# First expert of a mixture of experts: row numbers ahead of the gates, one-hots between the weights' second parts

## The chip, the cores and the metric

The kernel runs on one core of a Trainium2 chip. A core has TensorE (PE), VectorE (DVE), ScalarE (ACT), GpSimd (POOL) and SyncE (SP), each with its own line of instructions that it works off in order, and 16 DMA engines that move data between HBM and the core's own memory (SBUF). Matrix products go to PSUM. The metric is the device time of the whole program in microseconds (us).

## What is computed

A diffusion backbone of two layers over 1024 tokens of width 1024. Layer 0 mixes tokens by attention, layer 1 by a Fourier transform; behind each stands a mixture of experts: each token picks one of four groups, and in it two of eight experts, so there are 32 experts and 2048 pairs of a token and an expert. Cut to that part:

```python
lg = xt @ w_rg + b_rg                       # 4 groups
g_sel = argmax(lg); p_grp = max(softmax(lg))
le_sel = (xt @ w_re + b_re) of group g_sel  # 8 experts
top_l, top_i = top_k(le_sel, 2)
gate = p_grp * softmax(top_l)
y[t] = sum over both e of gate * ((silu(x @ w1[e]) * (x @ w3[e])) @ w2[e])
x = x + g2 * y
```

All inputs are float32.

## The kernel before, in words

**Gathering an expert's rows.** The routing (`route_part`, L1078) leaves for every token and expert a place among that expert's tokens (`posb`), and a table `val` of five small numbers: two make up the token's row number (written early by GpSimd), three are the gate weight in three bfloat16 parts (VectorE, L1168 to L1171). `slot_index` (L1206) makes for one expert a one-hot matrix `oneh` of 1024 tokens by 104 slots (VectorE, L1216), multiplies it with `val` on TensorE (`pi`, L1219), and reads from the product the row numbers (`row`, `idx`) and the gates (`gate`). With `idx` GpSimd gathers 104 rows of the normed input H from HBM (`xg`, L1333). H is stored row tile by row tile on SyncE's queue, the last tile on ScalarE's (L1024). `xin` (L1337) transposes the rows (`pt`) and splits them into a first part `xh` (ScalarE) and a second part `xl` = `pt` - `xh` (VectorE, L1346).

**Weights.** Each expert has twelve weight quarters of 128 x 1024 numbers: four of w1, four of w3, four of w2. A quarter comes by SyncE's queue, is split by ScalarE into `wh` (L1264) and by VectorE into `wl` = weight - `wh` (L1269); there are five buffers for split quarters, and quarters are split three ahead of their use. Every product is then three matmuls (`mm3`): first parts (L211), `wl` with `xh` (L212), `wh` with `xl` (L213). Before the experts start, eleven halves of weight matrices are loaded and the first five quarters' `wh` are cast; their five `wl` are left for later ("late", L1279) and done by `finish_late`.

**The start of the experts** (`phase_moe`). `prep(0, 1)` makes the one-hot, row numbers and gate of expert 0 and its gather is issued. TensorE does 14 products of no use on the one-hot meanwhile (`keep_warm`, L218). A `behind` marker on GpSimd behind the gather holds VectorE back from the next: `finish_late` does the five late `wl`, `prep(1, 3)` the one-hots and row numbers of experts 1 to 3, then `xin` of expert 0. Expert 0's products for w1 (`h1`) and w3 (`h3`) follow; between them `xin` of expert 1 and `prep(4, 4)`. VectorE multiplies both (`gg`, L1367). Expert 1 then runs like every later one: h1, `gg` of expert 0 transposed and split (`gh`, `gl`), w2's product of expert 0 (`py`), h3.

The order within an engine's line comes from the order in which the program issues, which a scheduler changes by its own estimate; `issue_after` and `behind` tie an instruction behind another one. The gain V of layer 1's first norm (`next_norm`, L1411, V = (V + 1) * norm gain) is computed ahead of layer 0's experts. `route_extra` (around 924 us) looks for experts with more than 104 rows.

Of the kernel before, what the change touches and what calls it, by code (L numbers as in the profile page):

```python
# [209 lines left out]
def mm3(nc, out, lh, ll, wh, wl, start, stop):  # L210
    nc.tensor.matmul(out, lh, wh, start=start, stop=False)  # L211
    nc.tensor.matmul(out, lh, wl, start=False, stop=False)  # L212
    nc.tensor.matmul(out, ll, wh, start=False, stop=stop)  # L213

# [861 lines left out]
def route_part(g, m, n0, n1, buf=None, pt_=None):  # L1076
# [6 lines left out]
    with ExitStack() as st:  # L1083
        if buf is None:
            wk = g.pool(st, "ra", 1)
            pp = g.pool(st, "rap", 1, psum=True)
# [53 lines left out]
        V.tensor_copy(m.posb[:, ns], m.posm[:, ns])  # L1140
        ex = T("ex", N, NG)
        V.tensor_tensor(ex, lg[:, :, 0], gm.to_broadcast([P, N, NG]), OP.subtract)
        nc.scalar.activation(ex, ex, AF.Exp)
        V.tensor_sub(m2, m2, m1)
        V.tensor_mul(m2, m2, ohg)
        e2 = T("e2", N)
        V.reduce_sum(e2, m2, axis=AX.X)
        nc.scalar.activation(e2, e2, AF.Exp)
        for oh in (oh1, oh2):
            V.tensor_mul(oh, oh, ohg[:, :, :, None].to_broadcast(sh))  # L1150
        o1, o2 = (oh.rearrange("p t g e -> p t (g e)") for oh in (oh1, oh2))
        pg = T("pg", N)
        V.reduce_sum(pg, ex, axis=AX.X)
        V.reciprocal(pg, pg)
        w1 = T("w1", N)
        V.tensor_scalar(w1, e2, 1.0, None, OP.add)
        V.reciprocal(w1, w1)
        V.tensor_mul(w1, w1, pg)
        w2 = T("w2", N)
        V.tensor_mul(w2, w1, e2)  # L1160

        val = m.val[:, ns]
        sh = [P, N, NE]
        V.tensor_mul(o1, o1, w1[:, :, None].to_broadcast(sh))
        V.tensor_mul(o2, o2, w2[:, :, None].to_broadcast(sh))
        G = o1
        V.tensor_add(G, o1, o2)
        V.tensor_copy(val[:, :, :, 2], G)  # L1168
        V.tensor_sub(G, G, val[:, :, :, 2])
        V.tensor_copy(val[:, :, :, 3], G)  # L1170
        V.tensor_sub(val[:, :, :, 4], G, val[:, :, :, 3])  # L1171
        if n1 == NT:
            m.cnt = m.one.tile([P, NE], F32, name="cnt")
            V.tensor_copy(m.cnt, cnt)

# [29 lines left out]

def slot_index(g, m, wk, pp, n, posm, val, tag):  # L1206

    nc = g.nc
    b = NE // 4 - 1 if n > 3 else 1
    pi = pp.tile([CAP, n, 5], F32, name="pi")  # L1210
    for e in range(n):
        oh = wk.tile([P, NT, CAP], BF, name="oneh", bufs=3)
        pe = posm(e)
        for t0, t1 in ((0, NT),) if n > 1 else ((0, NT - 2), (NT - 2, NT)):
            sh = [P, t1 - t0, CAP]
            nc.vector.tensor_tensor(oh[:, t0:t1], g.jrow[:, None, :].to_broadcast(sh),  # L1216
                                    pe[:, t0:t1, None].to_broadcast(sh), OP.is_equal)
        for t in range(NT):
            i = nc.tensor.matmul(pi[:, e], oh[:, t], val(e, t), start=(t == 0), stop=(t == NT - 1)).ins  # L1219
    g.slots = i, oh.rearrange("p t c -> p (t c)")[:, :512]  # L1220
    row = wk.tile([CAP, n], F32, name="row" + tag, bufs=1)
    nc.vector.tensor_scalar(row, pi[:, :, 1], float(SEQ), None, OP.add)
    idx = wk.tile([CAP, n], I32, name="idx" + tag, bufs=b)
    g.idx = nc.vector.tensor_add(idx, row, pi[:, :, 0]).ins
    gate = wk.tile([CAP, n], F32, name="gate" + tag, bufs=b)
    nc.vector.reduce_sum(gate, pi[:, :, 2:5], axis=AX.X)
    return idx, gate


class Moe:  # L1230
# [44 lines left out]

    def finish_late(self):

        for l, t, h in self.late:
            self.vsub = self.g.nc.vector.tensor_sub(l, t, h).ins  # L1279
        self.late = []  # L1280
        self.feed()
# [55 lines left out]
    def xin(self, xg):  # L1337
        g, nc = self.g, self.g.nc
        xh = self.wk.tile([P, KD, CAP], F32R, name="xh")
        xl = self.wk.tile([P, KD, CAP], F32R, name="xl")  # L1340
        for q in range(2):
            pt = self.ps.tile([P, 4, CAP], F32, name="pt", bufs=2)
            for j in range(4):
                nc.tensor.transpose(pt[:, j], xg[:, (4 * q + j) * P:(4 * q + j + 1) * P], g.ident[:CAP, :CAP])  # L1344
            nc.scalar.copy(xh[:, 4 * q:4 * q + 4], pt)  # L1345
            nc.vector.tensor_sub(xl[:, 4 * q:4 * q + 4], pt, xh[:, 4 * q:4 * q + 4])  # L1346
        return xh, xl
# [4 lines left out]
    def mm(self, out, x, piece, i, n=0, kpp=2):  # L1352

        hv, lv = (t.rearrange("p (k n) -> p k n", k=kpp)[:, :, n * 512:(n + 1) * 512] for t in piece)
        for j in range(kpp):
            k = i * kpp + j
            mm3(self.g.nc, out, x[0][:, k], x[1][:, k], hv[:, j], lv[:, j], k == 0, k == 4 * kpp - 1)

# [43 lines left out]
    def next_norm(self):  # L1402

        g, nc = self.g, self.g.nc
        if self.l:
            with g.tc.issue_after(self.piece):
                bcast_row(g, self.V, g.a["final_norm"].rearrange("(o d) -> o d", o=1), nc.sync)
            return
        bcast_row(g, self.G2, g.a["norm_mix"][1:2], nc.sync)
        bcast_row(g, self.V, g.mod[1][0:1, D:2 * D], nc.sync)  # L1410
        nc.vector.scalar_tensor_tensor(self.V, self.V, 1.0, self.G2, OP.add, OP.mult)  # L1411
        self.tab = {}

    def table(self, n):
# [25 lines left out]
def phase_moe(g, mo, after=None, fin=None):  # L1440
# [4 lines left out]
    with mo.st as st:  # L1445
# [12 lines left out]

        prep(0, 1)
        gather(0)  # L1460
        first = mo.last.ins
        with tc.issue_after(g.slots[0]):
            keep_warm(g, mo.psum("py", 2), g.slots[1], NWARM[0])
# [687 lines left out]
```

## Time and profile before

| | us |
|---|---|
| median of 3 runs | 2293.72 |
| lowest and highest | 2289.53, 2297.05 |
| the profiled execution, by the device's own time | 2295.38 |
| its span, first to last instruction | 2293.6 |
| TensorE busy in it | 2115.9 (92%) |
| VectorE busy in it | 1905.6 (83%) |
| ScalarE, GpSimd busy in it | 1341.7 (58%), 1014.5 (44%) |

The mean granted clock of TensorE is 0.964 of full. Layer 0's experts begin near 856 us of the span, layer 1's near 1643. A row of a timeline begins with the start and the busy time in us, then engine, line, operation, result <- inputs, shape, and the count where like instructions in a row are printed as one; in brackets stands the idle time ahead of it and what ended that. Engines overlap the end of one operation with the start of the next, so the busy time of one is some tenths longer than its share in a row.

### The profile page before, as it was taken

The numbers are of one execution on the slowest core, as the hardware profiler recorded it, in microseconds if no ns is written. First come the engines' busy times: TensorE is split into PE (matmuls) and PEld (weight loads), VectorE is DVE, ScalarE is ACT, GpSimd is POOL, SyncE is SP. The second block draws the span as 40 slices with busy tenths as digits, with TensorE's granted clock in tenths as the row PEclk, the third lists the DMA queues.
The fourth block names the chain that finished last, engine by engine and source line by source line (L and its number), as shares of the span: only waits on it lengthen the run. The fifth ranks groups of instructions, "written<-read, shape, count | busy, mean of one in ns | idle before, by whom it ended". The sixth has DMA issues, their size and how long they took to land. (4 is left out here: it accounts for less than half of the span.)

```text
span 2293.6 us, 29597 instructions
## 1 busy us (share of the span) xinstructions
PE 2115.9 (92%) x10301; PEld 1435.9 (63%) x10301; DVE 1905.6 (83%) x2782; ACT 1341.7 (58%) x1745; POOL 1014.5 (44%) x546
## 2 busy tenths in 40 slices
PE   6899899999999869999999999799699999999993
PEld 3677454444545656677777776457476777777662
DVE  4878566666677889999999999656899999999995
ACT  4743444444444236777777777543487777776774
POOL 3322577777778532334433443313223334434433
PEclk9999899999999989999999999899899999999997
DMA  8545533534335778999999999654699999999995
GB/s 304 190 156 157 174 119 126 177 118 138 120 107 177 269 270 284 364 368 335 364 361 337 370 378 327 218 228 167 243 329 351 377 311 370 366 354 361 355 354 198
DMA packets 152070, 612.13 MB, mean 267 GB/s; under 512 B 26928, under 2 KB 43960, under 8 KB 105916
## 3 DMA queue, kind: packets, MB, share of 16 engines
q1 hardware_dynamic: 109628, 544.77, 64.3%
q0 software_dynamic: 24672, 54.40, 9.3%
q10 hardware_dynamic: 17616, 11.01, 1.5%
q8 instruction: 83, 1.36, 0.2%
q14 instruction: 71, 0.58, 0.1%
HBM read 557.47 MB, written 77.39 MB: 277 GB/s over the span
## 5 line engine op out<-in xcount | busy, mean ns | idle before, releaser
L212 PE MATMUL h<-wl,xh 128*104 128x512 f32 x1024 | 409.3, 400 | 16.5 <-DVE wl L1269 15.4
L211 PE MATMUL h<-wh,xh 128*104 128x512 f32 x1024 | 408.8, 400 | 0.5 <-ACT xh L1345 0.5
L213 PE MATMUL h<-wh,xl 128*104 128x512 f32 x1024 | 406.6, 397 | 0.0
L572 DVE TENSOR_REDUCE m<-sm 128x1 f32<-128x512 f32 x360 | 201.8, 593 | 107.6 <-PE sm L571 107.1
L1333 POOL DMA_INDIRECT xg<-H,idx x64 | 106.0, 1656 | 287.7 <-PE pt L1344 170.2
L212 PEld LDWEIGHTS h<-wl,xh 128*104 128x104 f32 x1024 | 173.4, 169 | 85.8 <-DVE wl L1269 24.3
L1264 ACT CAST wh<-raw 128x1024 fp32r<-128x1024 f32 x196 | 200.2, 1056 | 32.7 <-PE h L213 20.8
L1269 DVE TENSOR_TENSOR wl<-raw,wh 128x1024 fp32r<-128x1024 f32 x175 | 212.7, 1255 | 6.9 <-ACT wh L1264 6.8
L1269 DVE TENSOR_TENSOR wl<-wl,wh 128x1024 fp32r<-128x1024 f32 x163 | 211.0, 1323 | 2.5 <-ACT wh L1264 1.9
L211 PEld LDWEIGHTS h<-wh,xh 128*104 128x104 f32 x1024 | 173.3, 169 | 61.5 <-ACT xh L1345 0.9
L213 PEld LDWEIGHTS h<-wh,xl 128*104 128x104 f32 x1024 | 173.5, 169 | 60.7
L1388 POOL DMA_INDIRECT Xs<-y,idx x64 | 177.1, 2768 | 71.9 <-DVE y L1387 42.9
L1269 DVE TENSOR_TENSOR wl<-wh 128x1024 fp32r<-128x1024 f32 x157 | 206.4, 1337 | 3.0 <-ACT wh L1264 2.4
L1264 ACT CAST wh<-wh 128x1024 fp32r<-128x1024 f32 x180 | 186.3, 1054 | 38.2 <-PE h L213 26.7
L212 PE MATMUL py<-wl,gh 128*104 128x512 f32 x512 | 203.9, 399 | 0.1
L213 PE MATMUL py<-wh,gl 128*104 128x512 f32 x512 | 201.6, 396 | 0.5 <-DVE gl L1378 0.4
L1264 ACT CAST wh<-wl 128x1024 fp32r<-128x1024 f32 x172 | 178.4, 1055 | 34.7 <-PE h L213 24.8
L211 PE MATMUL py<-wh,gh 128*104 128x512 f32 x512 | 196.5, 402 | 2.0 <-ACT gh L1377 1.8
L1264 ACT CAST wh<-X 128x1024 fp32r<-128x1024 f32 x124 | 129.5, 1054 | 52.7 <-PE h L213 41.3
L1269 DVE TENSOR_TENSOR wl<-X,wh 128x1024 fp32r<-128x1024 f32 x113 | 141.4, 1283 | 4.2 <-ACT wh L1264 4.1
L1269 POOL TENSOR_TENSOR wl<-wh 128x1024 fp32r<-128x1024 f32 x23 | 67.3, 2926 | 166.3 <-issue 95.0
L571 PE MATMUL sm<-KS,qs 128*128 128x512 f32 x360 | 135.4, 383 | 0.0
(576 smaller groups left out, 4710.0 us busy)
## 6 DMA issues: line engine op xcount, KB each, us to landing
raw<-in_moe_w_dram SPq DMA_DIRECT2D x98, 1024.0 KB
wh<-in_moe_w_dram SPq DMA_DIRECT2D x90, 1024.0 KB
wl<-in_moe_w_dram SPq DMA_DIRECT2D x86, 1024.0 KB
qs<-in_moe_w_dram SPq DMA_DIRECT2D x96, 512.0 KB
raw<-in_w_mod_dram SPq DMA_DIRECT2D x43, 1024.0 KB
X<-in_moe_w_dram SPq DMA_DIRECT2D x37, 1024.0 KB
X<-in_moe_w_dram SPq DMA_DIRECT2D x50, 512.0 KB
QS<-qst ACTq DMA_DIRECT2D x32, 256.0 KB
```

The costliest lines, as they stand in the source:

```text
L211: nc.tensor.matmul(out, lh, wh, start=start, stop=False)
L212: nc.tensor.matmul(out, lh, wl, start=False, stop=False)
L213: nc.tensor.matmul(out, ll, wh, start=False, stop=stop)
L571: nc.tensor.matmul(ps[:, :kn], qs[:, h, qt * P:(qt + 1) * P], g.KS[:, g4, k0:k0 + kn], start=True, stop=True)
L572: nc.vector.reduce_max(m3[:, h, qt, b:b + 1], ps[:, :kn], axis=AX.X)
L1264: nc.scalar.copy(h, t)
L1269: i = (nc.gpsimd if pool else nc.vector).tensor_sub(l, t, h)
L1333: self.last = self.g.nc.gpsimd.indirect_dma_start(out=xg, out_offset=None, in_=self.H if src is None else src, in_offset=bass.IndirectOffs ...
L1388: return y, lambda: nc.gpsimd.indirect_dma_start(out=self.X, out_offset=bass.IndirectOffsetOnAxis(ap=idx, axis=0), in_=y, in_offset=None, ...
```

## The change

Six edits, all around the start of the experts.

1. In `route_part` the gate weights become a function of their own, called for the last stretch of tokens after the first gather is issued; the `cnt` copy goes to ScalarE. The routing's buffers stay open through the experts.
2. `slot_index` can make row numbers only (`rows_only`): a product with two columns of `val`, then `idx`; the gate comes from a second product with the other three columns, on the same one-hot.
3. `finish_late(2)` does two late `wl`, then come expert 0's gate and `prep(1, 3)`; the other three come behind `xl` of expert 0.
4. `prep(4, 4)` and the gather of expert 4 move from expert 0 to the start of expert 1.
5. `xin` of expert 1 moves from between h1 and h3 of expert 0 to behind its h3.
6. In layer 0, V is computed after expert 0's products, behind the newest `wl`.

```diff
-        ex = T("ex", N, NG)
...
+        def gates():
+            ex = T("ex", N, NG)
...
+            V.tensor_sub(val[:, :, :, 4], G, val[:, :, :, 3])
         if n1 == NT:
             m.cnt = m.one.tile([P, NE], F32, name="cnt")
-            V.tensor_copy(m.cnt, cnt)
+            nc.scalar.copy(m.cnt, cnt)
+            m.gates = gates
+        else:
+            gates()
...
-def slot_index(g, m, wk, pp, n, posm, val, tag):
+def slot_index(g, m, wk, pp, n, posm, val, tag, rows_only=False):
...
+    cs = slice(0, 2) if rows_only else slice(0, 5)
...
+    if rows_only:
+        def fin():
+            pi = pp.tile([CAP, n, 5], F32, name="pi")
+            collect(pi, 0, oh, slice(2, 5))
+            nc.vector.reduce_sum(gate, pi[:, :, 2:5], axis=AX.X)
+            return gate
+        return idx, fin
...
-        nc.vector.scalar_tensor_tensor(self.V, self.V, 1.0, self.G2, OP.add, OP.mult)
         self.tab = {}
+    def norm_gain(self):
+        self.g.nc.vector.scalar_tensor_tensor(self.V, self.V, 1.0, self.G2, OP.add, OP.mult)
...
-        prep(0, 1)
+        idx, gate = slot_index(g, m, mo.wk, mo.ps, 1, lambda e: m.posb[:, :, e], lambda e, t: m.val[:, t, e], "1", True)
+        info[0] = idx, None
         gather(0)
         first = mo.last.ins
+        m.gates()
...
         with behind(g, free, mybir.EngineType.DVE):
-            mo.finish_late()
+            mo.finish_late(2)
+            info[0] = idx, gate()
             prep(1, 3)
...
-        X = {0: mo.xin(xgs[0])}
+        with tc.issue_after(g.oneh):
+            X = {0: mo.xin(xgs[0])}
+        with tc.issue_after(mo.xl):
+            mo.finish_late()
         gather(GA)
...
+            if e == 1:
+                prep(IB)
+                gather(1 + GA)
...
-                if e + 1 < NE:
+                if 0 < e < NE - 1:
                     X[e + 1] = mo.xin(xgs[(e + 1) % GA])
-                if e == 0:
-                    with tc.issue_after(mo.vsub):
-                        prep(IB)
-                gather(e + 1 + GA)
+                if e:
+                    gather(e + 1 + GA)
...
                 if e == 0:
+                    with tc.issue_after(g.pe):
+                        X[1] = mo.xin(xgs[1])
+                    if not mo.l:
+                        with tc.issue_after(mo.vsub):
+                            mo.norm_gain()
                     mo.vectors()
```

How VectorE's line reads at three places, each before and after. First, layer 0, around the first one-hot (`aoh` holds the gate weights, L1168 to L1172 write their parts into `val`). Before:

```order
L1174 COPY cnt<-pre 128x32
L1168 CAST val<-aoh 128x64
L1169 TENSOR_TENSOR aoh<-aoh,val 128x64
L1170 CAST val<-aoh 128x64
L1171 TENSOR_TENSOR val<-aoh,val 128x64
L1216 TENSOR_TENSOR oneh<-jrow,posb 128x624
L1216 TENSOR_TENSOR oneh<-jrow,posb 128x208
L1222 TENSOR_SCALAR row_7359<-pi 104x1
L1224 TENSOR_TENSOR idx_7361<-row_7359,pi 104x1
L1226 TENSOR_REDUCE gate_7363<-pi 104x1
L1279 TENSOR_TENSOR wl<-raw,wh 128x1024 x4
```

After, in the same place of VectorE's line:

```order
L1169 CAST val<-aoh 128x64
L1231 TENSOR_TENSOR oneh<-jrow,posb 128x624
L1231 TENSOR_TENSOR oneh<-jrow,posb 128x208
L1170 TENSOR_TENSOR aoh<-aoh,val 128x64
L1171 CAST val<-aoh 128x64
L1236 TENSOR_SCALAR row_7331<-pi 104x1
L1172 TENSOR_TENSOR val<-aoh,val 128x64
L1238 TENSOR_TENSOR idx_7333<-row_7331,pi 104x1
L1300 TENSOR_TENSOR wl<-raw,wh 128x1024 x2
L1244 TENSOR_REDUCE gate_7335<-pi 104x1
L1231 TENSOR_TENSOR oneh<-jrow,posb 128x832 x3
```

The one-hot now stands ahead of three of the four operations on the gate weights, `cnt` is gone, and the gate is read behind two late `wl` rather than ahead of all five; the next three one-hots come after two `wl`.

Second, layer 0, VectorE behind the row numbers of experts 1 to 3 (`wl` of L1269, or L1290 after, are those split in turn, of L1300 the late ones). Before:

```order
L1269 TENSOR_TENSOR wl<-X,wh 128x1024
L1269 TENSOR_TENSOR wl<-qs,wh 128x1024
L1216 TENSOR_TENSOR oneh<-jrow,posb 128x832 x3
L1346 TENSOR_TENSOR xl<-pt,xh 128x416 x2
L1216 TENSOR_TENSOR oneh<-jrow,posb 128x832
L1269 TENSOR_TENSOR wl<-qs,wh 128x1024
L1222 TENSOR_SCALAR row_7549<-pi 104x4
L1269 TENSOR_TENSOR wl<-X,wh 128x1024
L1224 TENSOR_TENSOR idx_7551<-row_7549,pi 104x4
L1226 TENSOR_REDUCE gate_7553<-pi 104x4
L1269 TENSOR_TENSOR wl<-X,wh 128x1024 x2
L1367 TENSOR_TENSOR gg<-s,h_7558 104x512
```

After, VectorE's line from there on:

```order
L1300 TENSOR_TENSOR wl<-raw,wh 128x1024 x2
L1300 TENSOR_TENSOR wl<-X,wh 128x1024
L1290 TENSOR_TENSOR wl<-X,wh 128x1024
L1290 TENSOR_TENSOR wl<-qs,wh 128x1024 x2
L1290 TENSOR_TENSOR wl<-X,wh 128x1024
L1231 TENSOR_TENSOR oneh<-jrow,posb 128x832
L1290 TENSOR_TENSOR wl<-X,wh 128x1024 x2
L1388 TENSOR_TENSOR gg<-s,h_7499 104x512
L1367 TENSOR_TENSOR xl<-pt,xh 128x416 x2
L1436 SCALAR_TENSOR_TENSOR V<-V,G_7101 128x1024
L1231 TENSOR_TENSOR oneh<-jrow,posb 128x832 x3
L1290 TENSOR_TENSOR wl<-X,wh 128x1024
```

The three remaining late `wl` stand first, `xl` of expert 1 stands behind `gg`, and V stands here, ahead of three of the four one-hots for experts 4 to 7.

Third, layer 1, VectorE from the first one-hot on. Before:

```order
L1170 CAST val<-aoh 128x128
L1171 TENSOR_TENSOR val<-aoh,val 128x128
L1216 TENSOR_TENSOR oneh<-jrow,posb 128x624
L1216 TENSOR_TENSOR oneh<-jrow,posb 128x208
L1222 TENSOR_SCALAR row_15006<-pi 104x1
L1224 TENSOR_TENSOR idx_15008<-row_15006,pi 104x1
L1226 TENSOR_REDUCE gate_15010<-pi 104x1
L1279 TENSOR_TENSOR wl<-raw,wh 128x1024 x4
L1279 TENSOR_TENSOR wl<-qs,wh 128x1024
L1216 TENSOR_TENSOR oneh<-jrow,posb 128x832 x3
```

After, the same stretch of VectorE's line:

```order
L1171 CAST val<-aoh 128x128
L1172 TENSOR_TENSOR val<-aoh,val 128x128
L1231 TENSOR_TENSOR oneh<-jrow,posb 128x624
L1231 TENSOR_TENSOR oneh<-jrow,posb 128x208
L1236 TENSOR_SCALAR row_14988<-pi 104x1
L1238 TENSOR_TENSOR idx_14990<-row_14988,pi 104x1
L1300 TENSOR_TENSOR wl<-raw,wh 128x1024 x2
L1231 TENSOR_TENSOR oneh<-jrow,posb 128x832
L1244 TENSOR_REDUCE gate_14992<-pi 104x1
L1231 TENSOR_TENSOR oneh<-jrow,posb 128x832 x2
```

Here the operations on the gate weights stay ahead of the first one-hot; the late `wl` are split as in layer 0, with one of the next one-hots ahead of the gate.

## Rows read from the trace of the kernel before

**Rows 1.** Busy time by stretch: stretch, length, engines, granted clock, DMA share, GB/s

```profile
889.00:936.00 47.00, 47.00 (x225) 34.87 (x224) 46.70 (x61) 38.04 (x43) 15.71 (x8) 1.00 1.02 357
936.00:958.00 22.00, 18.73 (x103) 13.24 (x102) 22.00 (x28) 11.74 (x14) 4.74 (x3) 0.92 0.95 354
958.00:1200.00 242.00, 240.51 (x1210) 178.18 (x1209) 238.64 (x250) 188.25 (x212) 95.18 (x40) 1.00 0.99 357
```

**Rows 2.** SyncE's weight loads, 960 to 1400 us: waited for, us, times, longest

```profile
SPq L195 <- DVE wl L1269: 304.9, 144, 7.0
```

**Rows 3.** Timeline of VectorE, layer 0, 849 to 865 us

```profile
850.53 1.23 DVE L1411 SCALAR_TENSOR_TENSOR V<-V,G 128x1024 f32<-128x1024 f32 x1 [1.05 <-DMA V<-mod]
...
854.79 0.25 DVE L1168 CAST val<-aoh 128x64 bf16<-128x64 f32 x1
...
855.78 1.10 DVE L1216 TENSOR_TENSOR oneh<-jrow,posb 128x624 bf16<-128x624 bf16 x2
857.54 0.16 DVE L1222 TENSOR_SCALAR row<-pi 104x1 f32<-104x1 f32 x1 [0.67 <-PE pi L1219]
857.74 0.15 DVE L1224 TENSOR_TENSOR idx<-row,pi 104x1 int32<-104x1 f32 x1
...
860.05 4.63 DVE L1279 TENSOR_TENSOR wl<-raw,wh 128x1024 fp32r<-128x1024 f32 x4 [2.09 <-POOL behind L1465]
```

**Rows 4.** DMA queues, 854.5 to 855.5 us: packets, MB, share of 16 engines

```profile
q10 hardware_dynamic: 5, 0.01, 2.2%
```

**Rows 5.** Timeline of GpSimd, layer 0, the first gather

```profile
858.76 1.13 POOL L1333 DMA_INDIRECT xg<-H,idx  x1 [14.22 <-DVE gate L1226]
```

**Rows 6.** Timeline of VectorE, layer 0, 869 to 890 us

```profile
869.58 0.16 DVE L1222 TENSOR_SCALAR row<-pi 104x3 f32<-104x3 f32 x1 [0.45 <-PE pi L1219]
...
872.53 1.26 DVE L1269 TENSOR_TENSOR wl<-X,wh 128x1024 fp32r<-128x1024 f32 x1 [2.15 <-ACT wh L1264]
875.14 1.23 DVE L1269 TENSOR_TENSOR wl<-qs,wh 128x1024 fp32r<-128x1024 f32 x1 [1.35 <-ACT wh L1264]
...
882.88 0.16 DVE L1222 TENSOR_SCALAR row<-pi 104x4 f32<-104x4 f32 x1 [0.64 <-PE pi L1219]
...
888.24 1.22 DVE L1269 TENSOR_TENSOR wl<-wh 128x1024 fp32r<-128x1024 f32 x1
```

**Rows 7.** Timeline of TensorE, layer 0, 857 to 877 us

```profile
857.37 4.92 PE L218 MATMUL py<-oneh,onesb 128*104 128x512 bf16 x14
863.68 0.90 PE L1344 MATMUL pt<-ident,xg 104*128 104x104 f32 x8 [1.39 <-DMA xg<-H,idx]
...
869.40 0.73 PE L213 MATMUL h<-wh,xl 128*104 128x512 f32 x1
...
874.58 0.40 PE L213 MATMUL h<-wh,xl 128*104 128x512 f32 x1
...
876.66 0.39 PE L213 MATMUL h<-wh,xl 128*104 128x512 f32 x1
```

**Rows 8.** Busy time, granted clock and DMA share by stretch, as rows 1

```profile
856.00:861.50 5.50, 4.85 (x20) 2.85 (x21) 2.71 (x7) 0.00 (x0) 2.73 (x4) 0.56 0.86 335
869.00:872.00 3.00, 3.00 (x13) 2.25 (x13) 0.93 (x5) 0.55 (x1) 0.85 (x1) 0.50 0.51 210
```

**Rows 9.** Timeline of VectorE, layer 1, 1647 to 1676 us

```profile
1647.04 4.63 DVE L1279 TENSOR_TENSOR wl<-raw,wh 128x1024 fp32r<-128x1024 f32 x4 [2.14 <-POOL behind L1465]
...
1659.36 1.23 DVE L1269 TENSOR_TENSOR wl<-qs,wh 128x1024 fp32r<-128x1024 f32 x1 [2.30 <-ACT wh L1264]
1661.44 1.23 DVE L1269 TENSOR_TENSOR wl<-X,wh 128x1024 fp32r<-128x1024 f32 x1 [0.86 <-ACT wh L1264]
...
1675.48 0.58 DVE L1378 TENSOR_TENSOR gl<-pt,gh 128x416 fp32r<-128x416 f32 x1
```

**Rows 10.** Timeline of TensorE, layer 1, the warm-up

```profile
1644.30 5.68 PE L218 MATMUL py<-oneh,onesb 128*104 128x512 bf16 x14
```

**Rows 11.** The gathers' line, whole span: issue to landing

```profile
DMA to landing us min/median/max: 4.8/9.5/12.5
```

More of the change, by code (lines that the diff above doesn't have):

```diff
@@ L212, in mm3 @@
     nc.tensor.matmul(out, lh, wl, start=False, stop=False)
-    nc.tensor.matmul(out, ll, wh, start=False, stop=stop)
+    return nc.tensor.matmul(out, ll, wh, start=False, stop=stop).ins
 def keep_warm(g, out, rhs, n):
@@ L1084, in route_part @@
         if buf is None:
-            wk = g.pool(st, "ra", 1)
+            wk = g.pool(m.st, "ra", 1, side=None if m.l else "right")
             pp = g.pool(st, "rap", 1, psum=True)
@@ L1140, in route_part @@
         V.tensor_copy(m.posb[:, ns], m.posm[:, ns])
-        ex = T("ex", N, NG)
[L1142 to L1171, printed above, removed]
+        def gates():
+            ex = T("ex", N, NG)
+            V.tensor_tensor(ex, lg[:, :, 0], gm.to_broadcast([P, N, NG]), OP.subtract)
+            nc.scalar.activation(ex, ex, AF.Exp)
+            V.tensor_sub(m2, m2, m1)
+            V.tensor_mul(m2, m2, ohg)
+            e2 = T("e2", N)
+            V.reduce_sum(e2, m2, axis=AX.X)
+            nc.scalar.activation(e2, e2, AF.Exp)
+            for oh in (oh1, oh2):
+                V.tensor_mul(oh, oh, ohg[:, :, :, None].to_broadcast(sh))
+            o1, o2 = (oh.rearrange("p t g e -> p t (g e)") for oh in (oh1, oh2))
+            pg = T("pg", N)
+            V.reduce_sum(pg, ex, axis=AX.X)
+            V.reciprocal(pg, pg)
+            w1 = T("w1", N)
+            V.tensor_scalar(w1, e2, 1.0, None, OP.add)
+            V.reciprocal(w1, w1)
+            V.tensor_mul(w1, w1, pg)
+            w2 = T("w2", N)
+            V.tensor_mul(w2, w1, e2)
+            val = m.val[:, ns]
+            shg = [P, N, NE]
+            V.tensor_mul(o1, o1, w1[:, :, None].to_broadcast(shg))
+            V.tensor_mul(o2, o2, w2[:, :, None].to_broadcast(shg))
+            G = o1
+            V.tensor_add(G, o1, o2)
+            V.tensor_copy(val[:, :, :, 2], G)
+            V.tensor_sub(G, G, val[:, :, :, 2])
+            V.tensor_copy(val[:, :, :, 3], G)
+            V.tensor_sub(val[:, :, :, 4], G, val[:, :, :, 3])
@@ L1210, in slot_index, with collect @@
     pi = pp.tile([CAP, n, 5], F32, name="pi")
+    cs = slice(0, 2) if rows_only else slice(0, 5)
+    def collect(pi, e, oh, cs):
+        for t in range(NT):
+            i = nc.tensor.matmul(pi[:, e, cs], oh[:, t], val(e, t)[:, cs], start=(t == 0), stop=(t == NT - 1)).ins
+        return i
     for e in range(n):
@@ L1215, in slot_index @@
             sh = [P, t1 - t0, CAP]
[L1216 to L1219, printed above, removed]
+            g.oneh = nc.vector.tensor_tensor(oh[:, t0:t1], g.jrow[:, None, :].to_broadcast(sh),
+                                             pe[:, t0:t1, None].to_broadcast(sh), OP.is_equal).ins
+        i = collect(pi, e, oh, cs)
     g.slots = i, oh.rearrange("p t c -> p (t c)")[:, :512]
@@ L1274, in quarter, with finish_late @@
         return h, l
-    def finish_late(self):
-        for l, t, h in self.late:
+    def finish_late(self, n=NLATE):
+        for l, t, h in self.late[:n]:
             self.vsub = self.g.nc.vector.tensor_sub(l, t, h).ins
-        self.late = []
+        self.late = self.late[n:]
         self.feed()
@@ L1345, in xin @@
             nc.scalar.copy(xh[:, 4 * q:4 * q + 4], pt)
-            nc.vector.tensor_sub(xl[:, 4 * q:4 * q + 4], pt, xh[:, 4 * q:4 * q + 4])
+            self.xl = nc.vector.tensor_sub(xl[:, 4 * q:4 * q + 4], pt, xh[:, 4 * q:4 * q + 4]).ins
         return xh, xl
@@ L1356, in mm @@
             k = i * kpp + j
-            mm3(self.g.nc, out, x[0][:, k], x[1][:, k], hv[:, j], lv[:, j], k == 0, k == 4 * kpp - 1)
+            self.g.pe = mm3(self.g.nc, out, x[0][:, k], x[1][:, k], hv[:, j], lv[:, j], k == 0, k == 4 * kpp - 1)
     def hidden(self, h1, h3):
@@ L1420, in begin @@
         self.m = Ctx()
+        self.m.st = self.st
         self.m.one = self.g.one
```

## The prediction

> **What bounds the kernel now.** I read busy time by stretch first, then what the weight loads waited for, then VectorE's and TensorE's instructions one by one where the first layer's experts begin, and last the same place in layer 1. From 958 us on TensorE is busy 240.51 of 242 us and bounds, but from 936 to 958 it is busy only 18.73 of 22, while VectorE is busy 22.00 of 22, and from 889 to 936 both are full [rows 1]. So for about 70 us behind the start of the experts VectorE never rests: whatever moment it reaches at 889 is carried to 958, where TensorE takes over and carries it to the end. Weights are not what is late: SyncE's weight loads stand waiting for VectorE to free buffers, 304.9 us in the stretch read [rows 2]. The question is therefore how much earlier VectorE ends the thirteenth `wl` of each layer, the last one before the first `gl`.
>
> **Layer 0, up to the first gather.** VectorE stands 1.05 us for V's transfer, then computes V; its next operation (`boh`) starts 1.14 us after V does [rows 3]. V leaves this place: 1.05 + 1.14 = 2.19 us, less about 0.05 of ordinary spacing, so -2.15. The `cnt` copy goes to ScalarE (some 0.1, about the spacing of such small operations: `idx` follows the row number by 0.20) and of the four `val` operations three move behind the one-hot: that was at 855.78, `val` began at 854.79 and lasts 0.25 itself, so -0.74, and -0.84 with `cnt` [rows 3]. The one-hot would start near 852.85 and the row number, 1.76 us behind it (855.78 to 857.54), at 854.6. But the row tile's space is only free when the last store of H has landed, and the gather reads H as well: the queue of that store (ScalarE's, q10) still moves 5 packets in 854.5 to 855.5 us [rows 4], its last ones. So the row number comes at about 855.45, `idx` 0.2 later, and the gather, 1.02 us behind the start of `idx` now (857.74 to 858.76), at 856.65 in place of 858.76 [rows 3, 5]. Of the 2.9 us won on VectorE 2.1 arrive. The first `wl` follows the gather by 1.29 us (860.05 less 858.76), so it starts at 857.95.
>
> **Layer 0, from there to the thirteenth `wl`.** Now the thirteenth `wl` ends at 888.24 + 1.14 = 889.38 (four in a row take 4.63 with the last one's tail, so 1.14 each) [rows 3, 6]. From 860.05 this is 29.33 us, of which VectorE waits 0.45 for the product behind three row numbers, 2.15 and 1.35 for ScalarE's first parts, and 0.64 once more for a row number: 4.59 in all [rows 6], so 24.74 of work. The two waits for ScalarE (3.5 us) come from TensorE: the first L213, which uses `xl`, starts only at 869.40, behind five `wl` and three one-hots, so the five split buffers come free late. After the change the same one-hots and `xl` follow two `wl` rather than five; the other three fill the time in which buffers come free. V is added here, 1.14, so the work is 25.88. Three waits can be left: the row number's (0.45, unchanged); the buffers', 0 to 0.95: the first L213 would come at about 863.75, and if it runs at 0.43 us a product, as at 869.40, the fourth buffer is free about 1 us after VectorE wants it, while at 0.23 it is free in time [rows 7]; and the `xl` of expert 1, whose transposes now follow expert 0's last product, 0 to 1.0 (half of the 0.90 of the transposes, a cast and hand-overs, an estimated 0.8, less the `gg` beside them). I take 0.8 of the 2.4 possible, since the last 0.64 wait falls behind a `wl` that covers it, and the buffers' one holds only for a low clock. Then 857.95 + 25.88 + 0.8 = 884.65 against 889.38: **-4.7** (ends -3.1 and -5.5). The second parts that move behind `xl` release their raw buffers about 2.3 us later than now; eleven pieces are held, and loads are waiting for VectorE everywhere [rows 2], so this costs nothing unless the held pieces run out.
>
> The gate's own product runs on TensorE behind the 14 warm-up products. These now take 857.37 to 862.29 [rows 7]; with the one-hot 2.9 us earlier they end at about 859.4, eight small products follow, under 1 us (the eight larger transposes take 0.90 [rows 7]), so the sum is ready at 860.3, just when VectorE has done its two `wl` (857.95 + 2.3). I count no wait here, at most 0.5. Behind the gate in VectorE's line stand the three one-hots, and TensorE waits for those.
>
> TensorE's clock bears on the range. The granted clock is 0.50 from 869 to 872 us (1.2 GHz), behind a stretch of little work [rows 8]; the products, 0.43 us apart from 869.40 on (twelve to 874.58), are 0.23 apart, as at 2.4 GHz, behind it (nine to 876.66) [rows 7]. That costs about 12 x 0.2 = 2.4 us now. With 4.4 rather than 7.1 us between warm-up and the first L213 it may not fall; I count half of that.
>
> **Layer 1.** Here all `val` operations still stand ahead of the one-hot in VectorE's line; only `cnt` is gone, so the gather comes 0.1 earlier. From the first `wl` at 1647.04 to the first `gl` at 1675.48 is 28.44 us, of which 2.30 and 0.86 were waits for ScalarE [rows 9]; with some 0.65 for row numbers (0.45 and 0.64 in layer 0, less here, since these products begin nearer to the full clock) 3.8. V is not in this layer. Left are: the gate's wait, 0.5 (the warm-up starts at 1644.30, takes 5.68, then 0.9 for the small products: 1650.8 [rows 10]; VectorE stands ready after two `wl` and a one-hot, 1646.94 + 3.2 = 1650.15); a row number's, 0.2; buffers and `xl`, 0 to 1.65, of which I take 0.4. So -0.1 - 3.8 + 1.1 = **-2.8** (ends -1.5 and -3.3, and -3.9 if no wait is left).
>
> **Sum.** -4.7 - 2.8 = -7.5 us (ends -4.5 and -9.4). The profiled execution took 2295.38 us, its span 2293.6, so that one would be 2287.9; it lies 1.7 above the median of three, 2293.72. Against the median: **2286.2 us**. What a measurement can tell from no change is 0.3%, here 6.9 us, so the forecast lies just beyond that bound and much of its range within.
>
> **Rivals.** (1) The first gather lands late. It is the next thing due: VectorE reaches `xl` at about 863.1 (857.95 + two `wl` 2.3 + three one-hots 2.85), and the gather, issued at 856.65, has to land by 861.8 for transposes and cast (1.25) to be done (0.45 and 0.8, as above). Now TensorE waited 1.39 us for it and it landed 4.8 us after issue (863.68, less a hand-over, against 858.76), the shortest of all 64; the median is 9.5 [rows 7, 11]. At 4.8 it lands at 861.45, 0.35 to spare. Until 861.5 weights stream beside it, 0.86 of the engines' time in 856 to 861.5 [rows 8], and 2.1 us more of that stream now meet it. At the median, 866.15, `xl` waits 4.3 us in VectorE's line, with the late `wl` behind it; layer 0 gives 0.4, the whole -3.2: 2290.5. Against it speaks that now it met most of the same stream and landed in 4.8. The Trainium skill bears on this (DMA: Bandwidth & Descriptors, Queues, rings and completion order): each DMA engine takes turns between the queue rows that have work, a packet at a time, so a gather beside weights must share. By that rule the median landing, not 4.8, would hold, and the result would be this rival's; the trace bears it out in the steady stretches, where landings are twice as long, and not in the one that counts.
> (2) What is won is given back at expert 1. TensorE has no products for about 1 us while `xl` of expert 1 is made, the clock falls there as it did at 869, and 12 products at 0.43 again cost 2.4; if VectorE then waits for buffers as long, -7.5 + 2.4 = -5.1: 2288.6.
> (3) The change does in layer 1 nothing that it says: the gates stand ahead of the one-hot there anyway, and if the gate's wait and `xl` eat the rest, only layer 0 counts: -4.7, 2289.0.
> (4) Slower. With light work strewn between the first products (small products, one-hots, transposes), TensorE stays at 1.2 GHz through expert 0 and the first part of expert 1: 72 products x 0.2 = 14.4 us a layer where 2.4 is lost now. It decides where the extra exceeds the shift: beyond 24 slow products more in layer 0 the gain is gone, with 72 more in all the kernel is slower by over 6.9 us, and at 72 in each layer the total is 2 x 12 - 7.5 = +16.5: 2310.2. Against it: the dense stretch starts as dense as now, and there the products went from 0.43 to 0.23 us 5.2 us after the first L213 [rows 7].
>
> **Chances.** Forecast with its own range, 5.5 to 9.5 us gained: 0.75. Rival 1: 0.10, rival 2: 0.05, rival 3: 0.05, rival 4: 0.05. Within the forecast's range the part beyond 6.9 us is 2.6 of 4.0, so faster is 0.75 x 0.65 = 0.49; the rest of it and rivals 1 to 3 make 0.46 of no telling change; slower is rival 4, 0.05. The range runs from 2282 (9.5 gained and some 2 us of spread of the runs, which lay 2289.53 to 2297.05) to 2291.5 (rival 1 with 1 us of spread).
>
> **What would show it.** In layer 0: first gather at 856.6, first late `wl` at 858.0, first L213 near 863.8 and the thirteenth `wl` ended near 884.7; V between expert 1's `xl` and the next one-hots. In layer 1 the first L213 near 1653 and the thirteenth `wl` about 2.8 earlier than its layer's start would give. VectorE without rest behind that, to about 950 in layer 0. Wrong it would be by an `xl` that waits for the gather, by a wait of VectorE for ScalarE as long as now, or by a clock at half longer than 5 us after the first L213.

## The result

The changed kernel takes 2310.69 us (median of 5 runs, 2306.49 to 2313.31) beside 2293.63 us for the kernel before on the same chip (5 runs): a ratio of 1.0068, 95% interval 1.0049 to 1.0087. By the ratio it is slower by about 16 us (17.1 between the medians), where 7.5 us less were forecast. The profiled execution took 2309.48 us, its span is 2307.3 us, 13.7 more than before.

Stretches and clock, as rows 1 and 8: length, then PE, PEld, DVE, ACT and POOL busy, granted clock, DMA share, GB/s. The second is the one that did not exist before.

```profile
855.00:878.00 23.00, 20.51 (x110) 13.97 (x110) 18.78 (x34) 9.33 (x12) 11.77 (x5) 0.82 0.72 262
878.00:888.30 10.30, 0.14 (x2) 0.05 (x1) 2.24 (x3) 0.70 (x1) 4.73 (x3) 0.61 0.95 275
```

TensorE stands still for ten microseconds, and VectorE and ScalarE with it. In layer 1 it is the same: from 1673 to 1684 us TensorE is busy 0.11 of 11 us.

What TensorE waited for, first in layer 0 (855 to 960 us), then in layer 1 (1652 to 1760): waited for, us, times, longest.

```profile
PE pt L1365 <- DMA xg<-H,idx: 10.8, 2, 10.2
...
PE pt L1365 <- DMA xg<-H,idx: 11.0, 1, 11.0
```

Both are the transposes of expert 1, which wait for its gathered rows. Timeline of GpSimd, VectorE and TensorE around it, layer 0, in order of time:

```profile
858.79 1.13 POOL L1354 DMA_INDIRECT xg<-H,idx  x1 [12.61 <-DVE idx L1238]
...
864.40 0.90 PE L1365 MATMUL pt<-ident,xg 104*128 104x104 f32 x8 [0.60 <-DMA xg<-H,idx]
...
868.41 2.35 DVE L1300 TENSOR_TENSOR wl<-raw,wh 128x1024 fp32r<-128x1024 f32 x2
869.26 11.34 POOL L1354 DMA_INDIRECT xg<-H,idx  x1 [7.43 <-DVE idx L1238]
...
877.28 2.35 DVE L1290 TENSOR_TENSOR wl<-X,wh 128x1024 fp32r<-128x1024 f32 x2
877.72 0.40 PE L213 MATMUL h<-wh,xl 128*104 128x512 f32 x1
879.55 0.68 DVE L1388 TENSOR_TENSOR gg<-s,h 104x512 f32<-104x512 f32 x1
880.90 1.06 POOL L1354 DMA_INDIRECT xg<-H,idx  x1 [0.30 <-issue]
888.28 1.62 PE L1365 MATMUL pt<-ident,xg 104*128 104x104 f32 x8 [10.16 <-DMA xg<-H,idx]
...
889.78 1.29 DVE L1367 TENSOR_TENSOR xl<-pt,xh 128x416 fp32r<-128x416 f32 x2 [9.54 <-ACT xh L1366]
```

The gather of expert 1 occupies GpSimd for 11.34 us. Expert 0's gather takes 1.13, as in [rows 5], and the next one 1.06. It begins 0.85 us behind its `idx`, when VectorE has just begun nine `wl` and a one-hot without a pause, and it ends at 880.60, 1.05 us after `gg` has started. In layer 1 it takes 11.36 us and ends 1.06 us after `gg` (1663.94 to 1675.30; `gg` at 1674.24). The kernel before issued this gather while VectorE waited for ScalarE, in the 2.15 us of [rows 6], and TensorE had the rows in time. The change fills that wait with three late `wl`. That the wait was what let GpSimd start is shown by the experiments below.

A smaller part of the delay is the transfer of the rows, with the DMA engines busy 0.95 of the time. From the end of the issue to the transposes it is 7.7 us here (880.60 to 888.28); in the kernel before the rows had landed 4.9 us after the start of their issue of 1.08 us.

To set one execution beside another I count in each layer from the last normed row tile (VectorE's L1023): 845.90 us in layer 0 before, 847.54 after; 1633.60 and 1642.91 in layer 1.

| us from there | layer 0 before | after | layer 1 before | after |
|---|---|---|---|---|
| first gather issued | 12.87 | 11.25 | 12.11 | 12.12 |
| first L213 | 23.50 | 19.97 | 22.57 | 19.32 |
| `gg` of expert 0 | 40.61 | 32.01 | 39.01 | 31.33 |
| transposes of expert 1 | 30.99 | 40.74 | 29.28 | 40.98 |
| `gg` of expert 1 | 57.41 | 67.23 | 55.82 | 66.31 |
| `gg` of expert 15 | 319.00 | 328.14 | 317.49 | 327.07 |
| `gg` of expert 31 | 612.1 | 617.9 | 617.5 | 623.1 |

Expert 0 is done 8.6 and 7.7 us earlier, as the forecast wanted, and expert 1 comes 9.8 and 10.5 us later. Between experts 15 and 31 some 3 to 4 us are made up again in each layer; what makes them up was not examined.

### The profile page after: what moved, and what is told of

Same layout as the page of the kernel before. It is cut to its first block, busy times and chain, and to the rows that moved or that the text cites. A ratio compares the mean times of both kernels' runs of the same rounds, so it can differ in the third digit from the quotient of the medians.

```text
span 2307.3 us, 29625 instructions
## 1 busy us (share of the span) xinstructions
PE 2120.4 (92%) x10317; PEld 1439.7 (62%) x10317; DVE 1898.0 (82%) x2780; ACT 1344.1 (58%) x1747; POOL 1047.8 (45%) x546
## 4 chain that ended last, share of the span: by engine, by line
PE 56%; DVE 22%; DMA 11%; issue 6%; ACT 3%; POOL 2%; SPq 0%; POOLq 0%; ACTq 0%; DVEq 0%
DVE wl L1290 9%; PE h L212 6%; PE h L213 6%; PE h L211 6%; PE po L675 5%; PE sm L571 4%; PE st L669 3%; PE st L670 3%; PE py L212 3%; PE py L213 3%; PE py L211 3%; PE mm L211 2%; DMA xg<-H,idx 2%; PE mm L213 2%; PE mm L212 2%
## 5 line engine op out<-in xcount | busy, mean ns | idle before, releaser
L213 PE MATMUL h<-wh,xl 128*104 128x512 f32 x1024 | 405.9, 396 | 0.0
L1354 POOL DMA_INDIRECT xg<-H,idx x64 | 140.5, 2196 | 302.2 <-PE pt L1365 162.9
L1290 DVE TENSOR_TENSOR wl<-raw,wh 128x1024 fp32r<-128x1024 f32 x175 | 218.2, 1286 | 5.9 <-ACT wh L1285 5.6
L213 PEld LDWEIGHTS h<-wh,xl 128*104 128x104 f32 x1024 | 173.5, 169 | 61.3
L1290 DVE TENSOR_TENSOR wl<-wl,wh 128x1024 fp32r<-128x1024 f32 x163 | 205.4, 1288 | 2.4 <-ACT wh L1285 2.4
L213 PE MATMUL py<-wh,gl 128*104 128x512 f32 x512 | 201.6, 396 | 1.0 <-DVE gl L1399 1.0
L1290 DVE TENSOR_TENSOR wl<-wh 128x1024 fp32r<-128x1024 f32 x157 | 198.2, 1285 | 5.1 <-ACT wh L1285 4.8
L1409 POOL DMA_INDIRECT Xs<-y,idx x64 | 168.0, 2625 | 59.9 <-DVE y L1408 30.3
L1290 POOL TENSOR_TENSOR wl<-wh 128x1024 fp32r<-128x1024 f32 x23 | 69.8, 3033 | 168.2 <-issue 98.3
L1290 DVE TENSOR_TENSOR wl<-X,wh 128x1024 fp32r<-128x1024 f32 x113 | 139.4, 1266 | 1.0 <-ACT wh L1285 0.7
```

What stands on the lines that cost most here:

```text
L213: return nc.tensor.matmul(out, ll, wh, start=False, stop=stop).ins
L1290: i = (nc.gpsimd if pool else nc.vector).tensor_sub(l, t, h)
L1354: self.last = self.g.nc.gpsimd.indirect_dma_start(out=xg, out_offset=None, in_=self.H if src is None else src, in_offset=bass.IndirectOffs ...
L1409: return y, lambda: nc.gpsimd.indirect_dma_start(out=self.X, out_offset=bass.IndirectOffsetOnAxis(ap=idx, axis=0), in_=y, in_offset=None, ...
```

## The experiments

The theory after the result (A): GpSimd cannot start on the gather's descriptors, the entries that tell the DMA engines what to move, while VectorE runs operations with two inputs from SBUF back to back. Its rivals: the gather is long because the DMA queues are full of weights (B); the new place of expert 1's transposes is at fault (C). Each run has runs of the kernel before beside it on its chip; ratios are to those.

**Small operations between the late `wl`.**

```diff
         for l, t, h in self.late[:n]:
             self.vsub = self.g.nc.vector.tensor_sub(l, t, h).ins
+            if between is not None:
+                self.vsub = between().ins
...
-            mo.finish_late()
+            mo.finish_late(between=lambda: nc.vector.tensor_copy(win[:CAP], wps[:, :64]))
```

Here `wps` is the PSUM tile of the warm-up; the second run has `nc.vector.tensor_add(win[:CAP], wsb[:CAP], wsb[:CAP])`, with `wsb` in SBUF.

> The changed kernel, and behind each of the three late `wl` that stand behind `xl` of expert 0 one small VectorE copy (104x64) that reads PSUM and nothing of SBUF; its result is not used. Theory A (GpSimd cannot start writing the gather's descriptors while VectorE runs operations with two SBUF inputs back to back; it gets in at an idle moment or at an operation that reads PSUM): the gather of expert 1 takes 1 to 2.5 us on GpSimd in place of 11.3, TensorE's wait for it goes from 10.2 and 11.1 us to under 1 us in both layers, and the time falls by some 20 us to 2286 to 2291. Rival B (the gather is long because the DMA queues are full of weights): it stays near 11 us and the time near 2311, since the copies move no DMA. Rival C (the new place of expert 1's transposes is at fault): time near 2311 as well.

> As the run with the copies that read PSUM, but the three small operations (104x64) add an SBUF tile to itself: two inputs, both from SBUF. Theory A: no window for GpSimd, the gather of expert 1 takes 11 to 12 us again, time 2309 to 2313. If the gather gets in here too (1 to 2.5 us, time under 2295), then any break between two `wl` would do and theory A's kind of operation is wrong.

Measured: 2298.01 us beside 2297.10, ratio 1.0005 (0.9993 to 1.0018), with the copy from PSUM; 2299.09 us, 1.0004 (0.9986 to 1.0021), with the addition in SBUF. GpSimd and VectorE in layer 0, first of the run with PSUM, then of the run with SBUF:

```profile
872.07 1.32 POOL L1356 DMA_INDIRECT xg<-H,idx  x1 [9.29 <-DVE idx L1238]
...
872.35 0.22 DVE L1511 COPY win<-py 104x64 f32<-104x64 f32 x1
```

```profile
876.38 1.32 POOL L1356 DMA_INDIRECT xg<-H,idx  x1 [11.75 <-DVE idx L1238]
...
876.66 0.22 DVE L1511 TENSOR_TENSOR win<-wsb 104x64 f32<-104x64 f32 x1
```

In both the gather ends 1.04 us after the small operation has started, in all 1.32 us, and TensorE no longer waits for expert 1's rows. Three copies that move no data by DMA take away the whole loss, with the transposes in their new place, so B and C are out as its cause. But the second run should have kept GpSimd out and did not: the kind of operation in A was wrong. Of the gain of 20 us some 15 came, by the ratios: back to the time before and not below it.

**Which operation lets GpSimd in.**

```diff
-            wsb = mo.wk.tile([P, 64], F32, name="wsb", bufs=1)
+            pw, nw = (CAP, 512) if mo.l else (P, 64)
+            wsb = mo.wk.tile([P, nw], F32, name="wsb", bufs=1)
...
-between=lambda: nc.vector.tensor_add(win[:CAP], wsb[:CAP], wsb[:CAP])
+between=lambda: nc.vector.tensor_add(win[:pw], wsb[:pw], wsb[:pw])
```

> The changed kernel with three unused VectorE additions of an SBUF tile to itself between the late `wl`, as in the run with 104x64 from SBUF, but in layer 0 of 128x64 and in layer 1 of 104x512. If the length of the operation decides (a short one lets GpSimd in, a long one not), the gather of expert 1 takes 1 to 2.5 us in layer 0 and 7 us or more in layer 1, there up to the next PSUM-reading operation. If the number of partitions decides (104 lets it in, 128 not), the other way round: 7 or more in layer 0, 1 to 2.5 in layer 1. If both take 1 to 2.5 us, any operation that is not a `wl` or a one-hot of full size does.

Measured: 8.53 us in layer 0 (128x64), 1.34 in layer 1 (104x512); 2305.47 us in the one run, beside 2302.97. GpSimd and VectorE, layer 0 and then layer 1:

```profile
870.48 8.53 POOL L1356 DMA_INDIRECT xg<-H,idx  x1 [8.68 <-DVE idx L1238]
...
870.76 0.22 DVE L1512 TENSOR_TENSOR win<-wsb 128x64 f32<-128x64 f32 x1
879.59 2.36 DVE L1290 TENSOR_TENSOR wl<-X,wh 128x1024 fp32r<-128x1024 f32 x2 [1.53 <-ACT wh L1285]
...
1662.17 1.34 POOL L1356 DMA_INDIRECT xg<-H,idx  x1 [6.22 <-issue]
...
1662.45 0.68 DVE L1512 TENSOR_TENSOR win<-wsb 104x512 f32<-104x512 f32 x1
```

The partitions decide and not the length: three operations on 128 partitions left it standing until VectorE fell idle, 1.53 us ahead of 879.59; a long one on 104 let it in. A further run puts 128 partitions to the test from both sources:

```diff
-between=lambda: nc.vector.tensor_add(win[:CAP], wsb[:CAP], wsb[:CAP])
+between=lambda: (nc.vector.tensor_add(win, wsb, wsb) if mo.l else nc.vector.tensor_copy(win, mo.lastpt[:, 0, :64]))
```

> As the runs with small unused operations between the late `wl`, but both on 128 partitions and 64 wide: in layer 0 a copy that reads PSUM (the transposes of expert 0), in layer 1 an addition of an SBUF tile to itself. If an operation that leaves partitions 104 to 127 alone is what lets GpSimd in, and where it reads from makes no difference, the gather of expert 1 takes 7 us or more in both layers (up to the next idle moment or the next 104-partition operation) and the time is 2308 to 2316 beside 2297 to 2303 before. If reading PSUM also lets it in, it takes 1 to 2.5 us in layer 0 and 7 or more in layer 1.

Measured: 1.31 us in layer 0 (from PSUM), 8.55 in layer 1 (SBUF); 2311.40 us in the one run, beside 2301.57.

```profile
871.39 1.31 POOL L1356 DMA_INDIRECT xg<-H,idx  x1 [8.74 <-DVE idx L1238]
...
1661.08 8.55 POOL L1356 DMA_INDIRECT xg<-H,idx  x1 [5.83 <-issue]
```

So reading PSUM lets it in as well. What can keep the gather waiting is a row of operations with two SBUF inputs on all 128 partitions; an idle moment, an operation that reads PSUM, or one on 104 partitions lets it in, and it ends 0.95 to 1.06 us after that starts. Whether it is the 24 partitions left out, or only that their number changes from one operation to the next, these runs do not tell apart. An idle moment can be short: in layer 1 of the last run the gather ends 1 us after a gap of 0.03 us that VectorE left between the third and fourth of five `wl`. A later gather of the changed kernel bears the rule out; beside six `wl` in a row it ends 1.04 us after `y`, which reads PSUM, has started (GpSimd and VectorE, layer 0):

```profile
903.80 7.52 POOL L1354 DMA_INDIRECT xg<-H,idx  x1 [0.30 <-issue]
...
910.28 1.41 DVE L1408 SCALAR_TENSOR_TENSOR y<-py,gate,G 104x512 f32<-104x512 f32 x2
```

Only the start is held, not the whole issue: behind the small operations of the first two runs 0.9 of the 1.04 us pass beside the next `wl`. The rule is not complete. In the three runs with a marker, shown below, all twelve second and third gathers got in at seams, places where one full `wl` follows another without a gap (1.96 to 2.03 us each), where expert 1's gather of the changed kernel let nine seams pass. When a seam lets the gather in is open.

**Waiting for GpSimd on purpose.**

```diff
             gather(e)
+            if e == 1:
+                with tc.issue_after(mo.last.ins):
+                    passed = nc.gpsimd.memset(mo.wk.tile([P, 1], F32, name="passed", bufs=1), 0.0).ins
...
-            mo.finish_late()
+            with behind(g, passed, mybir.EngineType.DVE):
+                mo.finish_late()
```

A first version lacked the `issue_after`:

> The changed kernel; the three late `wl` behind `xl` of expert 0 also wait for a GpSimd memset that stands behind the gather of expert 1, so VectorE idles while that gather is issued. Theory A: the gather takes 1.1 us, VectorE waits about 2.1 us at that place in each layer, TensorE's wait for expert 1's rows is under 1 us, time 2289 to 2294. Rival B: the gather stays near 11 us and VectorE waits for it too, time 2325 or more.

Its memset was scheduled ahead of expert 0's gather (858.79 and 860.31 us), so it held nothing back: the run repeats the changed kernel (2316.29 us beside 2297.10, ratio 1.0084; a gather of 11.34 us) and tells nothing between A and B. With the marker in its place:

> The changed kernel; the three late `wl` behind `xl` of expert 0 wait for a GpSimd memset that now stands behind the gather of expert 1 in GpSimd's line; two one-hots of the next preparation come ahead of them. If the port theory holds: the gather waits out the two one-hots and then takes 1.1 us, some 2 to 3 us in all, VectorE idles 1 to 1.5 us, TensorE's wait for expert 1's rows is under 1.5 us in both layers, and the time is 2294 to 2300 beside 2297 of the kernel before. If the DMA queues were at fault, the gather stays at 7 us or more and the time above 2310.

> The kernel with the marker behind expert 1's gather once more, in more rounds: a ratio of 0.996 to 0.999 to the kernel before, with expert 1's gather of 2.0 to 2.1 us in both layers, if its gain is real; a ratio of 0.9995 or more if the first run's 0.9979 was chance.

Measured: 2297.78 us beside 2302.97, ratio 0.9979 (0.9964 to 0.9994); again 2298.60 beside 2301.57, 0.9987 (0.9976 to 0.9997). VectorE and GpSimd of the first of them, layer 0:

```profile
870.12 1.95 DVE L1231 TENSOR_TENSOR oneh<-jrow,posb 128x832 bf16<-128x832 bf16 x2
870.97 2.05 POOL L1354 DMA_INDIRECT xg<-H,idx  x1 [8.80 <-DVE idx L1238]
873.04 0.11 POOL L1504 MEMSET passed<- 128x1 f32 x1
873.18 2.36 DVE L1300 TENSOR_TENSOR wl<-raw,wh 128x1024 fp32r<-128x1024 f32 x2 [1.11 <-POOL passed L1504]
```

The gather waits out two one-hots and ends 0.95 us behind them; TensorE does not wait for expert 1's rows in either layer. For 1.11 us of an idle VectorE in each layer the kernel is faster than before by 3 to 5 us.

**Undoing parts of the change.**

```diff
-            mo.finish_late(2)
+            mo.finish_late()
...
-        with tc.issue_after(mo.xl):
-            mo.finish_late()
```

> The changed kernel with the split of the late `wl` undone: all five stand ahead of the gate and the one-hots of experts 1 to 3, as in the kernel before. The first L213 comes 3.0 to 3.4 us later than in the changed kernel. VectorE then waits for ScalarE's first parts soon behind the row numbers, at the latest behind the two one-hots that stand there, so the gather of expert 1 gets in after 2 to 4 us; TensorE's wait for its rows is under 3 us in place of 10 to 11, and the time is 2293 to 2300 beside 2297 to 2303 of the kernel before. If the split were not what closes GpSimd's way, the time would stay 14 us or more above the kernel before.

Measured: 2298.15 us beside 2301.57, ratio 0.9983 (0.9971 to 0.9996). The first L213 of layer 1 comes 22.62 us from the last row tile, 3.3 later than in the changed kernel; that of layer 0 comes at 20.75, only 0.8 later, with a first gather 1.0 us earlier (10.27). The gather of expert 1 takes 4.32 us in layer 0 and 2.07 in layer 1, and TensorE waits 4.2 us at most for rows in layer 0, more than the 3 expected, and not at all in layer 1. The split of the late `wl` is what closes GpSimd's way.

> The changed kernel with one part undone: expert 1's transposes stand between h1 and h3 of expert 0 again. Theory A: the gather gets in only at VectorE's next PSUM-reading operation or idle moment; `xl` of expert 1 now stands in VectorE's line ahead of `gg` and waits for the gather itself, so VectorE is idle sooner, the gather is done some 3 us earlier (after 8 to 9 us), TensorE waits 8 to 11 us in the middle of expert 0, and the time stays within 5 us of 2311. Rival C: without the move the wait is gone, time 2285 to 2292.

The edit puts `X[e + 1] = mo.xin(...)` of expert 0 back between h1 and h3. Measured: 2323.00 us beside 2297.10, ratio 1.0103 (1.0071 to 1.0135). The gather takes 6.99 us, up to the moment when VectorE runs out of work ahead of `xl`, and TensorE waits 10.2 and 12.0 us in the middle of expert 0. The wait is as expected, the time is not: it was to stay within 5 us of 2311. C is out here too. Whether the move of the transposes limited the damage can't be told: the interval overlaps with that of the repeat of the changed kernel on the same chip (1.0064 to 1.0105).

> The run with small copies from PSUM, with expert 1's transposes between h1 and h3 of expert 0 as in the kernel before. The gather is issued in time (1 to 2.5 us), but takes some 6 to 8 us to land, which is behind h1's end (some 5.6 us after the first L213, which comes 1.7 us ahead of the gather): TensorE waits 2 to 5 us for the rows in the middle of expert 0 in both layers, and the time is 2 to 6 us above the run with the copies alone. If the transposes' new place costs more than it brings, the time is 2 us or more below that run.

Measured: 2302.25 us beside 2302.97, ratio 0.9992 (0.9977 to 1.0007); TensorE waits 1.8 and 0.8 us at most, where 2 to 5 were expected. With the gather in time the place of the transposes makes no difference that can be told; the landing was quicker than I took it to be.

> The run with small copies from PSUM, with V computed ahead of layer 0's experts as in the kernel before. If V's move is worth what the prediction says (2.1 us of the path to the first gather less 1.14 us behind expert 0): the first gather of layer 0 comes 1 to 2 us later from the last normed row tile on, the end of layer 0 0 to 1.5 us later, layer 1 is unchanged, and the time lies within 2 us of the run with the copies.

> The run with the marker behind expert 1's gather, with V computed ahead of layer 0's experts as in the kernel before. The first gather of layer 0 comes 0 to 0.5 us later, since the last store of H sets it either way; V's 1.14 us leave VectorE's line behind expert 0. So the end of layer 0 is 0.6 to 1.2 us earlier than with the marker alone, layer 1 is unchanged, and the ratio to the kernel before is 0.997 to 0.999. If V's move was worth what the prediction said, it is 1 us later instead.

```diff
+        self.norm_gain()
         self.tab = {}
...
-                    if not mo.l:
-                        with tc.issue_after(mo.vsub):
-                            mo.norm_gain()
```

Measured: with the copies 2300.38 us beside 2302.97, ratio 0.9997 (0.9980 to 1.0015); with the marker **2296.41 beside 2301.57, ratio 0.9976 (0.9965 to 0.9986)**, the lowest ratio of all, though its interval overlaps with those of the marker with V behind. The first gather of layer 0 is issued 11.17 and 11.11 us from the last row tile with V ahead of it. Without, it is 11.25 in the changed kernel, 11.93 with the copies, 10.67 and 11.17 with the marker: V's move shows no gain there. Nor does its 1.14 us behind expert 0 show: `gg` of expert 15 comes at 318.1 with V first and at 317.8 and 318.0 with V behind.

## Why the prediction was wrong

**The step that failed** is a cost that was counted at nothing: "the other three fill the time in which buffers come free". The three late `wl` were moved behind the row numbers of experts 1 to 3, and the only thing asked of that time was whether VectorE could use it. What is queued behind `idx` on GpSimd, the gathers of experts 1 to 3, was not costed at all. In the kernel before these took 1.06 to 1.08 us because they could start in waits of VectorE. The timeline of GpSimd (and VectorE's `gg`) of the kernel before has a fifth gather, expert 4's, that shows such a cost:

```profile
871.15 1.08 POOL L1333 DMA_INDIRECT xg<-H,idx  x1 [9.35 <-DVE gate L1226]
872.53 1.06 POOL L1333 DMA_INDIRECT xg<-H,idx  x1 [0.30 <-issue]
...
885.06 2.47 POOL L1333 DMA_INDIRECT xg<-H,idx  x1 [10.08 <-PE h L213]
...
886.51 0.68 DVE L1367 TENSOR_TENSOR gg<-s,h 104x512 f32<-104x512 f32 x1
```

The one at 885.06 came while `wl` ran back to back and took 2.47 us; it ended 1.02 us after `gg` started, nearly the 1.05 of the changed kernel. The one at 872.53 started at the end of a wait, together with a `wl` [rows 6], and took 1.06 us beside it: the start is what is held. A late start of the gather would have been the fifth rival, with its place; its price would have been the length of the row of operations that the change puts there. TensorE was through with expert 0 at 877.95, 8.7 us after expert 1's gather of the changed kernel began (869.26); an issue of 1.1 us and the 7.7 us from its end to the transposes (880.60 to 888.28) would just have done, and an issue of 11.3 us is ten late.

The Trainium skill speaks of this, and I left it out: SBUF — State Buffer, "Who interferes with whom", says that a VectorE instruction with two SBUF inputs contends with a GpSimd instruction that reads SBUF, and that such contention is an exclusive lock. The trace agrees on the wait (11.34 us where 1.06 is the work), not on a lock in the other direction: the `wl` that started with the gather of 872.53 took 1.26 us [rows 6], where others take 1.22 to 1.23. The same section of the Trainium skill says that a probe did not see `tensor_tensor` stall a DMA; here the gather, which is a DMA, waits for `tensor_tensor` operations, and the measurement decides. What the number of partitions does is shown by these runs alone. The rule of the Trainium skill that was weighed instead, on DMA engines that take turns, stands beside the first rival, and that rival came in part: the transposes of expert 0 began 5.6 us after the issue (864.40 less 858.79) where it was 4.9 [rows 5, 7], and TensorE waited 0.60 us for the rows. In the other runs it waited 0.9 to 3.25 us for them in layer 0: 2.88 in the run with the marker, 2.09 in that with all five late `wl`. From issue to transposes it was 8.0 us at most, never the 9.5 of the median. Nor were the 4.8 us of [rows 11] the shortest of all 64 landings: in layer 1 of the same trace the transposes of expert 0 begin 4.1 us after the issue (1645.71 to 1649.82).

**The other steps.** The first gather of layer 0 was forecast 2.1 us earlier; it came 1.6 earlier. But 2.15 of the 2.9 won on VectorE were put down to V, and the runs with V first show none of that. What V leaves is taken by other waits: in the changed kernel's own trace VectorE waits 1.18 us for the router's products (L1039), and in the run with copies from PSUM and the two with the marker the row number waits 0.48, 0.68 and 1.01 us for the last store of H. The gate was to wait 0.5 us at most; it waited 1.39 in layer 0, since the warm-up took 6.14 us rather than 4.92 (the clock was at 0.50 from 859.5 to 861.5 us, before at 0.76 from 859.9 to 861.9), and nothing in layer 1. The first L213 was forecast 17.85 us from the last row tile in layer 0 (863.75) and came at 19.97; in layer 1 19.4 and 19.32. The clock did not fall ahead of expert 0 in the changed kernel: it stayed at 1.00 from 864 to 878 us, where before it was at half from 869 to 872 [rows 8].

**The size of the gain.** With the gather cured by small copies, the thirteenth `wl` of layer 1 ends 39.31 us from the last row tile (1674.95 + 1.14 - 1636.78) where it was 41.88: -2.6, forecast -2.8. VectorE, run with the copies, layer 1:

```profile
1674.95 1.23 DVE L1290 TENSOR_TENSOR wl<-X,wh 128x1024 fp32r<-128x1024 f32 x1
```

`gg` of expert 15 follows by -2.2; between two profiles of one kernel (the marker) that mark differs by 1.5 us in layer 1 and 0.2 in layer 0. So the sum of layer 1 holds, as far as these profiles can tell, once its missing term is paid. Layer 0 does not: there `gg` of expert 15 came at 321.5 with the copies (319.0 before) and at 315.5 in the run with V first. They differ in the clock at the first products. In the first the products for the row numbers ran at half:

```profile
868.26 2.20 PE L1223 MATMUL pi<-val,oneh 128*104 128x5 bf16 x24
...
870.50 0.16 DVE L1236 TENSOR_SCALAR row<-pi 104x3 f32<-104x3 f32 x1 [2.52 <-PE pi L1223]
```

and VectorE waited 2.52 us for them; in the second the clock was at 1.00 there and the wait 0.70. At the forecast's own mark, the end of the thirteenth `wl`, the forecast was -4.7. The run with the copies and V first reaches -4.1 there, within the forecast's ends (39.36 us from the last row tile, 43.48 before), and -3.5 at `gg` of expert 15; but V's place, a part of the change, is undone in it. At that mark the run with the copies alone has +1.8, those with the marker have -1.0 and -0.7. What decides at which clock the first products run was not settled.

**The rivals.** The fourth, TensorE at 1.2 GHz through expert 0, gave 2310.2 us, and 2310.69 was measured. That is chance: TensorE ran expert 0 at 1.00. Among the experts' first products the clock is at half only behind the ten idle microseconds, from 888 to 894 us. Its price was the right size and its mechanism was not there. The first cost 0.60 us here. The third did not come: with the gather cured, layer 1 gained nearly as much as was said. The second came, but as a consequence: TensorE without products at expert 1, and the clock falling there.

## What to carry to other kernels

An idle stretch of VectorE may be what another engine lives on. Before filling it, look up each instruction that GpSimd has in that stretch and how long the same one takes beside a busy VectorE; a gather's issue beside a row of operations with two SBUF inputs on all 128 partitions is the case to look for. The cure costs little: let VectorE wait for the issue (1.11 us a layer here, ratios 0.998 and 0.999 to the kernel before), or put an operation there that reads PSUM or leaves some partitions out (1.000 here).

## What was not expected of the hardware

The gather's issue on GpSimd, 1.06 us by itself, waited 10.3 us beside VectorE operations on 128 partitions with two SBUF inputs, `fp32` and `bf16` alike, of 64 to 1024 elements; the same addition on 104 partitions let it in after 0.28 us. The late rows then took 7.7 us more, with the DMA engines at 0.95 of their time from 878 to 888.3 us.
